# A two-layer hybrid trunk: the third weight sum formed from the second, low products last, block (0,0) summed in PSUM

## The chip, the cores and the metric

One core of one Trainium2 chip. The metric is the device time of one execution in microseconds, the median of the runs. One further execution was profiled; all rows of the trace are from it.

In the profile PE is TensorE's matmul, PEld its weight load, DVE is VectorE, ACT is ScalarE, POOL is GpSimd and SP is SyncE, which only issues transfers here.

## The reference, cut to what matters

Two layers over x, 512 tokens of 1024 numbers, in float32. Each layer is

```
x = x + concat(A, B, C) @ w_out                      # three kinds of attention heads
x = x + relu(RMSNorm(x) @ w_ff1)^2 @ w_ff2           # the feed-forward (FF) part
```

The change lies in the second line: w_ff1 is 1024 x 4096 and w_ff2 is 4096 x 1024, a matrix each per layer.

## The kernel before, in words

**Three products for one.** Float32 operands are split into a high part (rounded to the matmul type fp32r) and a low part (the rest). A product is hi·hi + hi·lo + lo·hi, three matmuls that add up in the same PSUM bank (`mm3`, L260 to L263). The weights are split on the chip: ScalarE copies the raw tile into `whi` (L203), VectorE subtracts that from the raw tile into `wlo` (L204). Both have three buffers (`HIB = 3`).

**Seven products for eight.** Most of the FF part uses a Strassen-Winograd scheme on 2 x 2 blocks, with seven block products. In FF1 the two of the eight slices of w_ff1 that come first (`NSTD = 2`) are done in the plain way, the other six with the scheme. FF2 uses it throughout, in four steps of two groups (`dg` = 0, 1). A *group* is the seven weight tiles A11, S1, S2, A12, S4, S3, A22 (`ORDER`) of 128 x 1024 numbers. There are 14 groups a layer, six of FF1 and eight of FF2, so 28 in all. Of the tiles, A11, A12 and A22 are blocks of the stored matrix (signs are put into the other operand). S1, S2, S3 and S4 are sums:

- S1 = block (1,0) + block (1,1): one plain load by SP's queue, then a second one by GpSimd's queue that adds in the transfer (`load_part`, L152 to L158)
- S2 = S1 + A11: VectorE, in place in A11's slot (L214)
- S4 = S2 + A12: VectorE, in A11's slot (L218)
- S3 = block (0,0) + block (1,0): a plain and an accumulating load
- A22 = block (1,1): a plain load

So a group has five plain loads, two accumulating ones and two VectorE sums, beside the seven splits.

**Jobs.** Each weight tile is a job in one list, in the order of use. `getjob` (L238) hands out the next; `prep_ahead` (L225) prepares up to three jobs ahead (sum if there is one, high part, low part), and `load_ahead` (L170) starts loads, in order, as long as the next one finds a free raw slot. In the FF part there are seven such slots of 128 x 1024 (three `raw`, four in `fraw`). A slot is given back by `drop`: S1's after S2's sum, A12's after S4's sum, A11's after S4's split, S3's and A22's after their own splits.

**The order in the FF part.** After the eight plain jobs, `ff_pairs` alternates a job of FF2 with a job of FF1. FF2 runs over steps, then over the seven products, then over the two groups; FF1 runs over slices, then over the seven products. So 28 jobs, two FF2 groups taken side by side and two FF1 groups one behind the other, are a round. FF1 is through before the last step of FF2, which runs its 14 jobs alone. The list scheduler of the language orders each engine's instructions when the program is built; each engine then works strictly in that order.

**One job on TensorE.** `prod` (L1126) runs over four row tiles and two column halves, with three matmuls of 256 columns each: 24 matmuls, and the low part of the weights comes in with the third.

**FF1's outputs.** `ff1_st` (L1219) does the seven products with banks X, Z and Y. The first product (A11) goes to X and is copied to `ct[:, 0]` in SBUF by ScalarE (L1222); X goes on adding. With the fourth product (A12) in Y, VectorE adds Y to `ct[:, 0]` (L1233), and ScalarE takes relu (L1176) and the square (L1177). Further differences (`n1_`, `n2_`, `tail_`, L1179 to L1190) and splits (L1167, L1168, L1172, L1173) by ScalarE and VectorE make FF2's moving operands. FF2 (`ff2`) adds its banks to xT with VectorE (`acc`, L1265), in the last step with a scaling by r2 (L1267). After layer 0 the next layer's first stage splits xT (L327, L328) and sums its squares (L319 to L323) for a matmul (L455) that takes their mean.

Of the kernel before, what the change touches and what calls it, by code (L numbers as in the profile page):

```python
# [15 lines left out]
AF = mybir.ActivationFunctionType  # L16
ALU = mybir.AluOpType
AX = mybir.AxisListType

P = 128  # L20
# [30 lines left out]
def trunk(ctx, tc, x, cols, rows, gate_w, tabs, w_in, w_out, w1, w2, out):  # L51
    nc = tc.nc
    V, A, G, T = nc.vector, nc.scalar, nc.gpsimd, nc.tensor
# [31 lines left out]
    def wt(tag, name):  # L85
        n, bufs = phase["tags"][tag]
        return phase["pool"].tile([P, n], F32, tag=tag, name=nm(name), bufs=bufs)
# [4 lines left out]
    def smt(n, name):  # L92
        return sm.tile([P, n], F32, tag=f"sm{n}", name=nm(name))

    def v3(a, d=HD):
        return a.rearrange("p (h d) -> p h d", d=d)
# [12 lines left out]
    def st_group(l, blocks):  # L109
        grp = {}  # L110
        for which, ij in (("A11", ((0, 0),)), ("S1", ((1, 0), (1, 1))), ("S2", ()), ("A12", ((0, 1),)), ("S4", ()),
                          ("S3", ((0, 0), (1, 0))), ("A22", ((1, 1),))):
            grp[which] = {"ap": [blocks[i, j] for i, j in ij], "which": which, "grp": grp, "n": 4, "w": 256, "ff": l,
                          "gate": None, "parts": 1}
        return grp
# [51 lines left out]
    def drop(jb):  # L167
        jb["ring"].append(jb.pop("raw"))
# [12 lines left out]
    def hilo():  # L181
        hi = wp.tile([P, D], F32R, tag="whi", name=nm("whi"), bufs=HIB)
        lo = wp.tile([P, D], F32R, tag="wlo", name=nm("wlo"), bufs=HIB)
        return hi, lo

    def prep_part(jb, part):
        if "hl" not in jb:
            jb["hl"] = hilo()
        hi, lo = jb["hl"]
        n, w, raw = jb["n"], jb["w"], jb["raw"]  # L190
        W = w
        if jb["gate"] is not None:
            l, k0 = jb["gate"]
            W = 268
            h3, l3, r3 = v3(hi[:, :n * W], W), v3(lo[:, :n * W], W), v3(raw[:, :n * w], w)
            A.activation(h3[:, :, :w], r3, AF.Copy)
            V.tensor_copy(h3[:, :, w:], gws[l][0][:, k0:k0 + n, :])
            V.tensor_tensor(l3[:, :, :w], r3, h3[:, :, :w], ALU.subtract)
            V.tensor_copy(l3[:, :, w:], gws[l][1][:, k0:k0 + n, :])
        else:  # L200
            m = n * w // jb["parts"]
            cs_ = slice(part * m, (part + 1) * m)
            A.activation(hi[:, cs_], raw[:, cs_], AF.Copy)  # L203
            V.tensor_tensor(lo[:, cs_], raw[:, cs_], hi[:, cs_], ALU.subtract)  # L204
        if part == jb["parts"] - 1:
            jb["res"] = [(hi[:, q * W:(q + 1) * W], lo[:, q * W:(q + 1) * W]) for q in range(n)]
            if jb["which"] in (None, "S3", "A22"):
                drop(jb)

    def prep_job(jb):  # L210
        which, g = jb["which"], jb.get("grp")
        if which == "S2":
            a = jb["raw"] = g["A11"]["raw"]
            V.tensor_tensor(a, g["S1"]["raw"], a, ALU.add)  # L214
            drop(g["S1"])
        elif which == "S4":
            a = jb["raw"] = g["A11"]["raw"]
            V.tensor_tensor(a, g["A12"]["raw"], a, ALU.add)  # L218
            drop(g["A12"])
        for part in range(jb["parts"]):  # L220
            prep_part(jb, part)
        if which == "S4":
            drop(g["A11"])

    def prep_ahead(i):  # L225
        while pos["prep"] < len(jobs):
# [11 lines left out]
    def getjob():  # L238
        i = pos["get"]
        if i > 0:  # L240
            jobs[i - 1].pop("res", None)
        load_ahead(i)
        prep_ahead(i)
        pos["get"] += 1
        return jobs[i]["res"]
# [14 lines left out]
    def mm3(o, sh, sl, mh, ml, first, last, skip=False):  # L260
        T.matmul(o, sh, mh, start=first, stop=False, skip_group_check=skip)  # L261
        T.matmul(o, sh, ml, start=False, stop=False, skip_group_check=skip)  # L262
        T.matmul(o, sl, mh, start=False, stop=last, skip_group_check=skip)  # L263
# [72 lines left out]
    def xop(op, lo):  # L336
        if op < 3:
            i, j = ((0, 0), (1, 0), (1, 1))[op]
            return xb(i, j, xl if lo else xh)
        return xbt["x"][:, ((op - 3) * 2 + lo) * 1024:((op - 3) * 2 + lo + 1) * 1024].rearrange(  # L340
            "p (k q) -> p k q", k=4)
# [54 lines left out]
    def headrms(zt, nh, name):  # L396
        sq = wt("tmp", "hsq")
        A.activation(sq[:, :nh * HD], zt, AF.Square)
        ss = smt(nh, name)
        V.tensor_reduce(ss, v3(sq[:, :nh * HD]), AX.X, ALU.add)  # L400
        v = smt(nh, name + "v")
# [42 lines left out]
    for l in range(L):  # L444
        last = l == L - 1
# [288 lines left out]
        def runA():  # L734
# [7 lines left out]
            def s1(c):  # L742
# [8 lines left out]
                for r in range(2):  # L751
                    V.tensor_reduce(v3(mx, 2)[:, :, r], v3(sc[r], 256)[:, :, :nk], AX.X, ALU.max)
                nmx = smt(4, "nmx")
# [321 lines left out]
        ct, bt = 0, 0  # L1075
# [19 lines left out]
        ct = v3(wt("ct", "ct"), S)  # L1095
# [11 lines left out]
        def bank():  # L1107
            return banks.popleft()
# [16 lines left out]

        def prod(bk, bh, bl, start):  # L1126
            ws = getjob()
            for kk in range(4):
                hi, lo = ws[kk]
                for f in range(2):  # L1130
                    c = slice(f * P, (f + 1) * P)
                    mm3(bk[:, f * 256:(f + 1) * 256], hi[:, c], lo[:, c], bh(kk), bl(kk), start and kk == 0 and f == 0,
                        kk == 3 and f == 1, True)

        def prod1(bk, op, start=True):
            bh, bl = xop(op, 0), xop(op, 1)
            prod(bk, lambda kk: bh[:, kk, :], lambda kk: bl[:, kk, :], start)
# [3 lines left out]
        def prod2(bk, s, op, start=True):  # L1141
            def pick(lo):
                def f(kk):
                    g = GU[s, kk // 2]
                    if op == 0:
                        return g["c"][:, lo, kk % 2, :]
                    tag, a = {1: ("b", 0), 2: ("b", 1), 3: ("n", 0), 4: ("n", 1), 5: ("t", 0), 6: ("t", 1)}[op]
                    return g[tag][lo][:, a, kk % 2, :]
                return f
            prod(bk, pick(0), pick(1), start)  # L1150
# [19 lines left out]
        def csplit(s, rr):  # L1170
            u = GU.setdefault((s, rr), {})["c"] = unit_for(s, False)
            A.activation(u[:, 0], q2(ct[:, 0]), AF.Copy)  # L1172
            V.tensor_tensor(u[:, 1], q2(ct[:, 0]), u[:, 0], ALU.subtract)  # L1173

        def act(a, src, sign):
            A.activation(ct[:, a], src, AF.Relu, scale=sign)  # L1176
            A.activation(ct[:, a], ct[:, a], AF.Square)  # L1177

        def n1_():  # L1179
            V.tensor_tensor(ct[:, 4], ct[:, 0], ct[:, 1], ALU.subtract)  # L1180

        def n2_(s, rr):
            V.scalar_tensor_tensor(ct[:, 5], ct[:, 3], -1.0, ct[:, 4], ALU.mult, ALU.subtract)
            V.tensor_tensor(ct[:, 1], ct[:, 3], ct[:, 1], ALU.subtract)
            gsplit(s, rr, "n", 4)

        def tail_(s, rr):
            gsplit(s, rr, "b", 2)
            V.scalar_tensor_tensor(ct[:, 2], ct[:, 5], -1.0, ct[:, 2], ALU.mult, ALU.subtract)
            gsplit(s, rr, "t", 1)  # L1190
# [26 lines left out]
                    yield  # L1217

        def ff1_st(s, rr):  # L1219
            X = bank()  # L1220
            prod1(X, 0)
            A.activation(ct[:, 0], X, AF.Copy)  # L1222
            yield
            Z = bank()
            prod1(Z, 3)
            A.activation(ct[:, 3], Z, AF.Copy)
            yield
            prod1(X, 4, False)
            A.activation(ct[:, 1], X, AF.Copy)
            yield  # L1230
            Y = bank()
            prod1(Y, 1)
            V.tensor_tensor(ct[:, 0], Y, ct[:, 0], ALU.add)  # L1233
            banks.append(Y)
            act(0, ct[:, 0], 1.0)
            csplit(s, rr)
            yield
            prod1(Z, 2, False)
            V.tensor_tensor(ct[:, 1], Z, ct[:, 1], ALU.add)
            banks.append(Z)  # L1240
            act(1, ct[:, 1], 1.0)
            n1_()
            yield
            prod1(X, 5, False)
            V.tensor_tensor(ct[:, 3], X, ct[:, 3], ALU.add)
            act(3, ct[:, 3], -1.0)
            n2_(s, rr)
            yield
            prod1(X, 6, False)
            act(2, X, -1.0)  # L1250
            banks.append(X)
            tail_(s, rr)
            yield
# [23 lines left out]
        def ff2(s):  # L1277
# [18 lines left out]
            for dg in range(2):  # L1296
                Y = bank()
                prod2(Y, s, 1)
                acc(s, dg, 0, 0, Y, True)
                banks.append(Y)  # L1300
# [102 lines left out]
```

## Time and profile before

| what | value |
|---|---|
| median of 3 runs | 1077.22 us (1075.41 to 1082.15) |
| profiled execution | 1074.93 us, span 1073.2 us |
| matmuls | 8376 |
| transfers that add, GpSimd's queue | 34 into `fraw`, 22 into `raw`, 512 KB each |
| HBM read | 147.86 MB |

A row of the profile that groups instructions reads: line, engine, operation, output <- inputs, shapes, count | busy us, mean ns of one | idle time of the engine before them, and what ended it. A row of the list of waits reads: who waited <- for whom: us in total, times, longest us. A row of the timeline: start, duration, instruction, and in brackets the idle time before it. A matmul's row lasts 0.28 us, but a new one starts every 0.11 us in the FF part, as they are pipelined. Starts of VectorE's neighbouring rows also lie closer than their lengths.

### The profile page before, as it was taken

To read this page: it belongs to the slowest core of one execution; us is meant where nothing else is said; L and a number is where in the kernel's file an instruction comes from. 1 tells how busy PE (TensorE), PEld (TensorE's weight loads), DVE (VectorE), ACT (ScalarE), POOL (GpSimd) and SP (SyncE) were. 2 spreads that over 40 slices of the span, in tenths; PEclk is the share of its full clock that TensorE was granted. 3 is DMA by queue.
4 is the path that set the end of the run, shared out by engine and by line. 5 is a ranking of instruction groups with operands and counts; after the bars stand their busy time and mean duration, and the time that the engine had idled before them with its cause. 6 is when DMAs were issued, how large, how long until landed. Compare 5 with 4: busy or idle time off the path is not lost.

```text
span 1073.2 us, 20903 instructions
## 1 busy us (share of the span) xinstructions
PE 1059.1 (99%) x8376; PEld 989.8 (92%) x8376; DVE 911.9 (85%) x1550; ACT 626.4 (58%) x1097; POOL 103.8 (10%) x154
## 2 busy tenths in 40 slices
PE   8999999999999999999999999999999999999998
PEld 8999977887999999999999998778789999999998
DVE  6696877899997997988977878688999889799897
ACT  5446655376666566566454567444765665576662
POOL 2030020101010010010001200101000100000100
PEclk8999999999999999999999999999999999999999
DMA  6533121145478588588435321213334866876872
GB/s 200 164 110 109 59 68 50 62 174 118 118 197 215 140 213 209 149 210 223 108 108 155 102 80 41 86 44 136 112 87 141 233 178 172 219 183 191 211 185 99
DMA packets 47346, 151.81 MB, mean 141 GB/s; under 512 B 5632, under 2 KB 8832, under 8 KB 47248
## 3 DMA queue, kind: packets, MB, share of 16 engines
q1 hardware_dynamic: 39184, 121.10, 33.8%
q0 software_dynamic: 8064, 29.36, 16.2%
q8 instruction: 66, 1.08, 0.4%
q14 instruction: 32, 0.26, 0.1%
HBM read 147.86 MB, written 2.13 MB: 140 GB/s over the span
## 4 chain that ended last, share of the span: by engine, by line
PE 80%; DVE 11%; ACT 3%; DMA 3%; issue 1%; SPq 0%; DVEq 0%; POOLq 0%
PE at L261 24%; PE at L263 24%; PE at L262 24%; DMA raw<-in_w_dram 3%; DVE wlo L204 2%; DVE rt L719 2%; PE at L849 1%; PE at L891 1%; PE at L874 1%; ACT whi L203 1%; ACT pe L762 1%; PE at L972 1%; DVE yg L1168 1%; DVE z L715 1%; DVE z L721 1%
## 5 line engine op out<-in xcount | busy, mean ns | idle before, releaser
L203 ACT ACTIVATE whi<-raw 128x1024 fp32r<-128x1024 f32 (+1 forms) x144 | 150.9, 1048 | 143.7 <-PE at L262 103.2
L204 DVE TENSOR_TENSOR wlo<-raw,whi 128x1024 fp32r<-128x1024 f32 (+1 forms) x144 | 173.8, 1207 | 41.2 <-ACT whi L203 40.7
L203 ACT ACTIVATE whi<-fraw 128x1024 fp32r<-128x1024 f32 x122 | 129.2, 1060 | 92.4 <-PE at L262 76.2
L261 PE MATMUL at<-yg,whi 128*128 128x256 f32 (+1 forms) x592 | 179.8, 307 | 0.0
L263 PE MATMUL at<-yg,wlo 128*128 128x256 f32 (+1 forms) x592 | 178.4, 301 | 0.0
L262 PE MATMUL at<-xhl,whi 128*128 128x256 f32 (+1 forms) x576 | 177.9, 309 | 0.0
L262 PE MATMUL at<-yg,whi 128*128 128x256 f32 (+1 forms) x560 | 169.6, 303 | 0.0
L261 PE MATMUL at<-whi,xhl 128*128 128x256 f32 (+1 forms) x576 | 164.1, 285 | 2.1 <-ACT whi L203 1.3
L262 PE MATMUL at<-wlo,xhl 128*128 128x256 f32 (+1 forms) x576 | 161.5, 280 | 0.3 <-DVE wlo L204 0.3
L263 PE MATMUL at<-whi,xhl 128*128 128x256 f32 (+1 forms) x576 | 161.5, 280 | 0.0
L261 PE MATMUL at<-xhl,whi 128*128 128x256 f32 (+1 forms) x512 | 161.1, 315 | 0.0
L263 PE MATMUL at<-xhl,wlo 128*128 128x256 f32 (+1 forms) x512 | 160.3, 313 | 0.0
L204 DVE TENSOR_TENSOR wlo<-fraw,whi 128x1024 fp32r<-128x1024 f32 x122 | 148.9, 1221 | 8.6 <-ACT whi L203 8.1
L261 PEld LDWEIGHTS at<-yg,whi 128*128 128x128 f32 x592 | 111.2, 188 | 5.6 <-issue 1.7
L263 PEld LDWEIGHTS at<-yg,wlo 128*128 128x128 f32 x592 | 111.2, 188 | 5.3
L262 PEld LDWEIGHTS at<-xhl,whi 128*128 128x128 f32 x576 | 108.0, 188 | 7.6 <-issue 0.5
L261 PEld LDWEIGHTS at<-whi,xhl 128*128 128x128 f32 x576 | 109.4, 190 | 3.2 <-ACT whi L203 1.6
L262 PEld LDWEIGHTS at<-wlo,xhl 128*128 128x128 f32 x576 | 109.5, 190 | 0.5 <-DVE wlo L204 0.5
L263 PE MATMUL at<-xbx,wlo 128*128 128x256 f32 x384 | 106.6, 278 | 3.4 <-DVE wlo L204 3.4
L263 PEld LDWEIGHTS at<-whi,xhl 128*128 128x128 f32 x576 | 109.3, 190 | 0.3 <-DVE xhl L328 0.3
L262 PEld LDWEIGHTS at<-yg,whi 128*128 128x128 f32 x560 | 105.3, 188 | 4.2 <-DVE yg L1002 0.5
L261 PE MATMUL at<-xbx,whi 128*128 128x256 f32 x384 | 106.1, 276 | 0.0
(286 smaller groups left out, 2423.1 us busy)
## 6 DMA issues: line engine op xcount, KB each, us to landing
fraw<-in_w_dram SPq DMA_DIRECT2D x90, 512.0 KB, 4.5
raw<-in_w_dram SPq DMA_DIRECT2D x66, 512.0 KB, 4.5
raw<-in_w_in_dram SPq DMA_DIRECT2D x34, 512.0 KB, 3.4
fraw<-in_w_dram POOLq DMA_DIRECT2D x34, 512.0 KB, 6.0
raw<-in_w_dram POOLq DMA_DIRECT2D x22, 512.0 KB, 7.9
raw<-in_w_out_dram SPq DMA_DIRECT2D x16, 512.0 KB, 3.4
rowb<-drow SPq DMA_DIRECT2D x16, 256.0 KB, 4.0
raw<-in_w_in_dram SPq DMA_DIRECT2D x12, 256.0 KB, 3.8
```

Of the source, the lines that this page charges most:

```text
L203: A.activation(hi[:, cs_], raw[:, cs_], AF.Copy)
L204: V.tensor_tensor(lo[:, cs_], raw[:, cs_], hi[:, cs_], ALU.subtract)
L261: T.matmul(o, sh, mh, start=first, stop=False, skip_group_check=skip)
L262: T.matmul(o, sh, ml, start=False, stop=False, skip_group_check=skip)
L263: T.matmul(o, sl, mh, start=False, stop=last, skip_group_check=skip)
L715: V.tensor_tensor(z10, z10, bc(rq), ALU.mult)
L719: V.tensor_tensor(r10[:, oo:oo + n, a:a + 32], z10[:, oo:oo + n, b:b + 32], tb(S_, n, a, a + 32), ALU.mult)
L721: V.tensor_tensor(zaq[t], ro[:, :640], rt[:, :640], ALU.add)
L762: A.activation(pe[:, u, :nk], sc[u % 2][:, (u // 2) * 256:(u // 2) * 256 + nk], AF.Exp, bias=nmx[:, u:u + 1], accum_out=ssum[:, u:u + 1])
L849: T.matmul(sp[:, :nk], qTB[rs, pr, n * P:(n + 1) * P], kTB[rs, pr, :nk], start=True, stop=False)
L874: T.transpose(pt[:, b * P:(b + 1) * P], scs[r][:, b * P:(b + 1) * P], ident)
L891: T.matmul(pobs[pr][r * 64:(r + 1) * 64, n * P:(n + 1) * P], zbv[b][:, h * 64:(h + 1) * 64], ps[r][:, b * P:(b + 1) * P], start=b == 0, st ...
```

## The change

S3 is no longer loaded. As S2 = (0,0) + (1,0) + (1,1), VectorE subtracts block (1,1) from S2, in A11's slot, which is held until S3's split. Block (1,1) is A22's tile, so its load moves up to S3's place in the list, and job A22 loads nothing. S4's sum goes into A12's slot in place of A11's, since S2 is still wanted. `prod` does the high part's 16 matmuls first, then the low part's 8. In `ff1_st`, ScalarE copies X to bank Y, and the A12 product adds to it there; VectorE's addition goes.

```diff
@@ st_group
-                          ("S3", ((0, 0), (1, 0))), ("A22", ((1, 1),))):
+                          ("S3", ((1, 1),)), ("A22", ())):
@@ prep_part
-        n, w, raw = jb["n"], jb["w"], jb["raw"]
+        n, w, raw = jb["n"], jb["w"], jb.get("src", jb.get("raw"))
...
-            if jb["which"] in (None, "S3", "A22"):
+            if jb["which"] is None:
                 drop(jb)
@@ prep_job
-        if which == "S2":
-            a = jb["raw"] = g["A11"]["raw"]
-            V.tensor_tensor(a, g["S1"]["raw"], a, ALU.add)
-            drop(g["S1"])
-        elif which == "S4":
-            a = jb["raw"] = g["A11"]["raw"]
-            V.tensor_tensor(a, g["A12"]["raw"], a, ALU.add)
-            drop(g["A12"])
+        last = None
+        if which:
+            a = g["A11"].get("raw")
+            jb["src"] = a if which in ("S2", "S3") else jb["raw"] if "raw" in jb else None
+            if which == "S2":
+                V.tensor_tensor(a, g["S1"]["raw"], a, ALU.add)
+                drop(g["S1"])
+            elif which == "S4":
+                jb["src"], last = g["A12"]["raw"], g["A12"]
+                V.tensor_tensor(jb["src"], jb["src"], a, ALU.add)
+            elif which == "S3":
+                V.tensor_tensor(a, a, jb["raw"], ALU.subtract)
+                last = g["A11"]
+            elif which == "A22":
+                jb["src"], last = g["S3"]["raw"], g["S3"]
         for part in range(jb["parts"]):
             prep_part(jb, part)
-        if which == "S4":
-            drop(g["A11"])
+        if last:
+            drop(last)
@@ prod
-            for kk in range(4):
-                hi, lo = ws[kk]
-                for f in range(2):
-                    c = slice(f * P, (f + 1) * P)
-                    mm3(bk[:, f * 256:(f + 1) * 256], hi[:, c], lo[:, c], bh(kk), bl(kk), start and kk == 0 and f == 0,
-                        kk == 3 and f == 1, True)
+            for i in range(2):
+                for kk in range(4):
+                    for f in range(2):
+                        c, o = slice(f * P, (f + 1) * P), bk[:, f * 256:(f + 1) * 256]
+                        w = ws[kk][i][:, c]
+                        T.matmul(o, w, bh(kk), start=start and i == kk == f == 0, stop=i == 1 and kk == 3,
+                                 skip_group_check=True)
+                        if i == 0:
+                            T.matmul(o, w, bl(kk), start=False, stop=False, skip_group_check=True)
@@ ff1_st
-            X = bank()
+            X, Y = bank(), bank()
             prod1(X, 0)
-            A.activation(ct[:, 0], X, AF.Copy)
+            A.activation(Y, X, AF.Copy)
...
-            Y = bank()
-            prod1(Y, 1)
-            V.tensor_tensor(ct[:, 0], Y, ct[:, 0], ALU.add)
+            prod1(Y, 1, False)
+            act(0, Y, 1.0)
             banks.append(Y)
-            act(0, ct[:, 0], 1.0)
```

## The prediction

> **What bounds the kernel now.** I read the page's busy table first, then the list of waits, then busy time by stretches, and last the timeline at one stall. An FF *job* is one weight tile of 24 matmuls; seven jobs make a group; a *round* is two FF2 groups and two FF1 groups taken in turn, 28 jobs.
>
> ```profile
> span 1073.2 us, 20903 instructions
> ...
> PE 1059.1 (99%) x8376; PEld 989.8 (92%) x8376; DVE 911.9 (85%) x1550; ACT 626.4 (58%) x1097; POOL 103.8 (10%) x154
> ```
>
> TensorE is idle for 14 us of 1073. The waits of TensorE, then those of the engines that feed it:
>
> ```profile
> PE at L263 <- DVE wlo L204: 3.4, 4, 1.1
> PE at L261 <- ACT whi L203: 1.3, 1, 1.3
> ```
> ```profile
> ACT whi L203 <- PE at L262: 179.4, 140, 4.2
> ...
> DVE wlo L204 <- ACT whi L203: 48.8, 73, 4.8
> ...
> ACT whi L203 <- DMA raw<-in_w_dram: 12.5, 4, 5.0
> ...
> DVE raw L214 <- DMA raw<-in_w_dram: 3.6, 3, 1.3
> ```
>
> The largest wait of TensorE is for low parts (wlo), 3.4 us in four places. ScalarE, which makes the high parts, waits 179 us for TensorE to free a buffer: the preparation normally runs ahead and is held back by TensorE. The stretches:
>
> ```profile
> 270.00:280.00 10.00, 9.36 (x82) 9.16 (x81) 9.72 (x11) 8.80 (x10) 0.00 (x0) 1.00 0.00 0
> ```
> ```profile
> 350.00:360.00 10.00, 8.95 (x79) 8.75 (x79) 8.67 (x10) 5.59 (x7) 0.00 (x0) 1.00 0.53 112
> 430.00:440.00 10.00, 8.97 (x79) 8.78 (x78) 10.00 (x11) 5.64 (x7) 0.86 (x1) 1.00 0.40 119
> 800.00:810.00 10.00, 9.35 (x82) 9.15 (x81) 9.71 (x12) 8.33 (x10) 0.00 (x0) 1.00 0.03 9
> ```
> ```profile
> 356.50:434.00 77.50, 76.47 (x673) 76.28 (x673) 68.12 (x73) 48.61 (x59) 6.93 (x8) 1.00 0.73 191
> ...
> 500.00:545.00 45.00, 45.00 (x396) 44.87 (x395) 44.45 (x56) 26.29 (x32) 2.26 (x3) 1.00 0.45 115
> ...
> 810.00:1068.00 258.00, 258.00 (x2267) 257.72 (x2266) 228.13 (x246) 153.87 (x181) 21.69 (x25) 1.00 0.69 186
> ```
>
> Columns: length, then busy time of TensorE, its weight loads, VectorE, ScalarE, GpSimd, clock, DMA share, GB/s. The first four rows hold the four stalls. The last row is almost the whole second FF stage without an idle moment of TensorE: 258/2267 = 0.114 us a matmul, 2.73 us a job. The fifth row is one round: VectorE is busy 68.1 of 77.5 us, so 9.4 us are free. In the sixth, the end of the first FF stage, VectorE is full. So TensorE's matmul count sets the time, the change leaves that count alone, and only stalls can be won or made.
>
> **The stalls and the late low parts.** One stall, on TensorE and on VectorE:
>
> ```profile
> 355.15 0.28 PE L262 MATMUL at<-xbx,whi 128*128 128x256 f32 x1
> 356.48 0.39 PE L263 MATMUL at<-xbx,wlo 128*128 128x256 f32 x1 [1.05 <-DVE wlo L204]
> ```
> ```profile
> 349.17 1.22 DVE L204 TENSOR_TENSOR wlo<-fraw,whi 128x1024 fp32r<-128x1024 f32 x1
> 351.73 1.23 DVE L214 TENSOR_TENSOR raw<-raw,raw 128x1024 f32<-128x1024 f32 x1 [1.33 <-DMA raw<-in_w_dram]
> 352.87 1.22 DVE L1168 TENSOR_TENSOR yg<-ct,yg 128x1024 fp32r<-128x1024 f32 x1
> 354.00 0.68 DVE L1265 TENSOR_TENSOR xT<-xT,at 128x512 f32<-128x512 f32 x1
> 354.60 0.69 DVE L1189 SCALAR_TENSOR_TENSOR ct<-ct 128x512 f32<-128x512 f32 x1
> 355.20 1.22 DVE L204 TENSOR_TENSOR wlo<-fraw,whi 128x1024 fp32r<-128x1024 f32 x1
> ```
>
> VectorE held a sum (L214) that stood waiting for a load, then FF1's bookkeeping, and only then the low part that the third matmul of the job needs. The high part was there: two matmuls of the job ran. Start to start the stall is 356.48 - 355.15 = 1.33 us where 0.11 is normal: 1.2 us. For all four: idle 3.4 plus, each, the 0.28 - 0.114 = 0.17 that the row's length overlaps: **4.05 us**. No stall is over 1.2 us.
>
> With low products last, TensorE needs the low part at the 17th matmul and not the 3rd: 14 x 0.114 = 1.59 us later, more than the worst lateness. I therefore take -4.05 us. Bounds: 0, if what is added on VectorE makes the low parts later by as much, and -4.05, since the FF stages hold no other stall. The high buffer's last reader becomes matmul 16 and not 23, so ScalarE may start 0.8 us earlier; it is ahead already, and I price that at 0.
>
> **VectorE's added and removed work.** Durations by line, first in the round above, then over the run:
>
> ```profile
> L204 DVE TENSOR_TENSOR wlo<-fraw,whi 128x1024 fp32r<-128x1024 f32 x17 | 20.8, 1221 | 1.2 <-ACT whi L203 1.1
> ...
> L214 DVE TENSOR_TENSOR fraw<-fraw 128x1024 f32<-128x1024 f32 x3 | 3.7, 1224 | 0.6 <-DMA fraw<-in_w_dram 0.5
> ...
> L1233 DVE TENSOR_TENSOR ct<-at,ct 128x512 f32<-128x512 f32 x2 | 1.4, 692 | 0.4 <-PE at L263 0.2
> ```
>
> The new subtraction has the shape of L214: 1.22 us, and 1.14 from start to start where such instructions follow each other (349.17 to the next was a wait; 351.73 to 352.87 is 1.14). There are 28 groups (14 a layer): +32 us. The removed addition L1233 runs 12 times, 0.69 us, 0.60 start to start (354.00 to 354.60): -7 us. A round gets 4 x 1.14 - 2 x 0.60 = +3.4 us against 9.4 free; with the 1.2 us stall gone the round is shorter and 4.8 us stay free. Beside TensorE, so 0 on the path, while it is spread. A job's low part is normally ready well before its job, as high copies start when TensorE frees the buffer of three jobs back: that leaves 2 x 2.73 - 1.06 (copy) - 1.22 = 3.2 us, and now 1.59 more. That cover hides four such subtractions in a row; without it each would cost its 1.14 us. S3's preparation becomes VectorE, ScalarE, VectorE in a chain, as S2's and S4's are, which cause no wait of TensorE by themselves.
>
> **Loads, slots, queues.**
>
> ```profile
> fraw<-in_w_dram SPq DMA_DIRECT2D x90, 512.0 KB, 4.5
> ...
> fraw<-in_w_dram POOLq DMA_DIRECT2D x34, 512.0 KB, 6.0
> raw<-in_w_dram POOLq DMA_DIRECT2D x22, 512.0 KB, 7.9
> ```
> ```profile
> L158 POOL DMA_DIRECT2D fraw<-in_w_dram x34: 856/865/1013, 244.1 to 1029.1; - x34
> ...
> DMA to landing us min/median/max: 3.1/5.5/10.4
> ```
>
> A group's five plain loads become four and its two accumulating ones become one: 28 of 56 issues leave GpSimd's queue and 28 leave SP's. TensorE never waits for a load directly, so they win 0; the stall above began with a load, but an S1 one, which stays. In exchange A11's slot is held until S3 and block A22's slot until A22. Counting the ring of seven slots through the job order, FF2's second group now finds the slot for its S3 load 4 jobs ahead (6 before), the others 6 or 7: 4 x 2.73 = 10.9 us, against a median landing of 4.5 and a longest of 10.4. I price it at 0; the bounds are 0 and the rival below.
>
> [...]
>
> **Block (0,0) in PSUM.** X is still copied once by ScalarE, into another bank; the addition leaves VectorE; relu reads PSUM.
>
> ```profile
> L1222 ACT ACTIVATE ct<-at 128x512 f32<-128x512 f32 x12 | 6.9, 578 | 0.0
> ```
>
> A write to PSUM by ScalarE is not in these rows; from the nearest, 0.58 us to SBUF, I take 0.58 (bounds 0 and twice that), off the path. The bank is held from FF1's first job to its fourth: FF1 has three and FF2 five, all eight, but in the order of the jobs no bank is reused sooner than three jobs (8.2 us) after its last reader, a 0.68 us addition. Price 0.
>
> **The end of the first FF stage.** VectorE has no room from 500 to 545. The last two groups add 2 x 1.14 = 2.3 us there. What is late next:
>
> ```profile
> 543.78 0.68 DVE L1267 TENSOR_TENSOR xT<-xT,r 128x512 f32<-128x512 f32 x1
> ...
> 548.56 3.73 DVE L323 TENSOR_TENSOR accs<-accs,sq 128x512 f32<-128x512 f32 x5
> ```
> ```profile
> 552.68 0.50 PE L455 MATMUL at<-ones_m,accs 128*128 128x1 f32 x4
> ```
>
> The last scaling frees the buffer in which the next layer's squares are summed; that sum ends at 552.3 and TensorE reads it at 552.7, 0.4 us of margin. Shifted by 2.3, TensorE stands 1.9 us at L455, once. Bounds 0 (the planner may put the scaling ahead of low parts) and 2.3. I take **+1.9**. At the very end nothing is due:
>
> ```profile
> 1065.69 0.69 DVE L1265 TENSOR_TENSOR xT<-xT,at 128x512 f32<-128x512 f32 x1 [1.30 <-PE at L263]
> ```
>
> There VectorE waits for TensorE again, 1.3 us twice.
>
> **Sum.** -4.05 + 1.9 = -2.15 us. The profiled execution took 1074.93 us (span 1073.2 and 1.7 around it): 1072.8. The median of the runs is 1077.22, 2.3 above it; on that scale, **1075.0 us**.
>
> **Rivals.** *The stalls only move*: VectorE's order is planned anew, another sum stands ahead of a low part, and nothing is won: 1077. For it: four stalls came from that order; against: 1.59 us of new cover. *The whole gain*: no stall at L455, 1073.2. *VectorE's queue stands behind loads*, the slower side: VectorE works in order, and the new subtraction waits for block A22's landing with everything queued behind it (low parts, FF2's additions). It decides from a mean of 4.8/4 = 1.2 us a subtraction on. At 2 us, a round loses 4 x 2 - 4.8 = 3.2, six rounds 19 us: 1096. For it: L214 waited 1.2 us on average, and S3 loads have made ScalarE wait up to 5.0; against: the load is now plain, and 10.9 us ahead at the least. [...]
>
> **How the numbers follow.** Forecast 0.50, whole gain 0.15, stalls move 0.20, port lock 0.02, VectorE behind loads 0.11, and 0.02 for a gain that I do not see. 1% (10.8 us) is about what a measurement of this kernel can tell from no change: faster by that 0.02, same 0.87, slower 0.11. Low end: the whole gain, 1073.2, less the 1.8 by which the fastest run shown lies under the median: 1071. High end: no gain at the slowest run, 1082.2, and the start of the loads' rival (1.5 us a subtraction: 1.2 x 6 = 7): 1084.
>
> **What would show it.** Right: no wait of TensorE for wlo in the FF stages; 28 accumulating issues; VectorE about 25 us busier; a wait of TensorE at the L455 matmuls near 1.9 us. Wrong: waits of the new subtraction for DMA above 1.2 us on average, or FF stretches with under 87 matmuls in 10 us.

## The result, and the profile after

The changed kernel takes **1093.01 us** (median of 6 runs, 1084.09 to 1095.9). Six runs of before beside it give 1076.32 us (1071.6 to 1082.15). The quotient of these medians is 1.0155; the ratio, which here and below leaves out runs more than 1.5% above the fastest of their kernel, is 1.0127 with a 95% interval of 1.0085 to 1.0169. That is slower by 1.3%, where 1075.0 us and a range of 1071 to 1084 were forecast. The profiled execution has a span of 1093.0 us, 19.8 more than before's 1073.2.

The page's busy table:

```profile
span 1093.0 us, 20783 instructions
...
PE 1067.9 (98%) x8376; PEld 998.5 (91%) x8376; DVE 930.6 (85%) x1566; ACT 623.4 (57%) x1097; POOL 77.6 (7%) x126
```

The edit itself is all there: 16 more VectorE instructions (28 subtractions less 12 additions), 28 fewer GpSimd issues, as many matmuls as before. TensorE's busy time cannot show what was lost, as the rows overlap (0.28 us long, a new one every 0.113 us in the FF stages). The list of TensorE's waits shows it (who <- for whom: us in total, times, longest):

```profile
PE at L1140 <- DVE wlo L204: 13.0, 4, 4.9
```

Before had 3.4 us for low parts, four times, 1.1 at most. There are still four places, but now up to 4.9 us each. VectorE's own waits say why the low parts are late:

```profile
DVE raw L217 <- DMA fraw<-in_w_dram: 14.7, 2, 7.6
...
DVE raw L217 <- DMA raw<-in_w_dram: 9.7, 2, 4.9
```

L217 is the sum S2 (L214 before), an instruction that the change did not touch in substance. It waited 3.6 and 0.5 us before and waits 24.4 us now. The new subtraction (L223) waits for no transfer at all. VectorE around the first of the four waits:

```profile
341.45 1.22 DVE L204 TENSOR_TENSOR wlo<-raw,whi 128x1024 fp32r<-128x1024 f32 x1
350.30 1.23 DVE L217 TENSOR_TENSOR raw<-fraw,raw 128x1024 f32<-128x1024 f32 x1 [7.63 <-DMA fraw<-in_w_dram]
...
353.24 1.23 DVE L1178 TENSOR_TENSOR gx<-ct,gx 128x1024 fp32r<-128x1024 f32 x1
354.39 2.35 DVE L204 TENSOR_TENSOR wlo<-fraw,whi 128x1024 fp32r<-128x1024 f32 x2
```

The same place before, from the low part of the same FF2 job A11 on. The prediction's rows of 349.17 (a low part) and 351.73 (the sum in question) follow these:

```profile
342.62 1.23 DVE L204 TENSOR_TENSOR wlo<-raw,whi 128x1024 fp32r<-128x1024 f32 x1 [0.29 <-ACT whi L203]
...
345.61 1.22 DVE L204 TENSOR_TENSOR wlo<-fraw,whi 128x1024 fp32r<-128x1024 f32 x1
```

Before, two low parts (345.61 and 349.17) stood between A11's low part and this sum. After the change the sum stands directly behind A11's low part, ahead of those two. The other three long waits are of the same kind: each is at the S2 sum of FF2's first group, in its second or third step, and each of these sums stands two low parts earlier than before. The load that it needs came no later than before. GpSimd issued its adding transfer in the changed kernel (first row) 1.8 us earlier than before (second row):

```profile
339.18 0.86 POOL L158 DMA_DIRECT2D fraw<-in_w_dram  x1 [1.99 <-DMA fraw<-in_w_dram]
```
```profile
341.02 0.87 POOL L158 DMA_DIRECT2D raw<-in_w_dram  x1 [2.26 <-DMA raw<-in_w_dram]
```

From issue to landing it took 11.0 us after the change and 10.7 before; why it takes so long at this place stays open. VectorE works in order, so it stood at the sum for 7.63 us, and the two low parts behind it came at 354.39. TensorE, in the job that wanted the first of them:

```profile
350.50 0.28 PE L1143 MATMUL at<-xhl,whi 128*128 128x256 f32 x1
355.66 1.73 PE L1140 MATMUL at<-xhl,wlo 128*128 128x256 f32 x8 [4.88 <-DVE wlo L204]
357.19 0.41 PE L1140 MATMUL at<-xhl,whi 128*128 128x256 f32 x1
357.40 0.41 PE L1143 MATMUL at<-xhl,whi 128*128 128x256 f32 x1
...
359.53 0.28 PE L1143 MATMUL at<-yg,whi 128*128 128x256 f32 x1
```

All 16 matmuls of the high part are done, as the new product order wants it, and still the low part is 5 us away. Behind the pause the matmuls start 0.21 us apart instead of 0.113 until 359.5. The stretches of TensorE (length, busy and rows, clock, DMA share, GB/s) show that and one thing more:

```profile
300.00:350.00 50.00, 50.00 (x443) 1.00 0.58 156
...
356.10:359.50 3.40, 3.40 (x18) 0.50 0.00 0
360.20:430.00 69.80, 69.80 (x595) 1.00 0.48 135
448.00:545.00 97.00, 97.00 (x826) 1.00 0.38 114
```

The granted clock fell to one half for 3.4 us after this pause, and again after the one of 4.56 us at 893 us; the pauses of 2.07 and 2.35 us had no such stretch. And from 360 to 545 us, but for some 9 us behind the second pause, a matmul took 97.0/826 = 0.1174 us, though the clock is 1.00 and nothing waits; ahead of the first pause it was 50.0/443 = 0.1129. (From start to start in the timeline it is 0.1178 and 0.1133; these two are used below.)

So the 19.8 us are, by an estimate from this one execution: pauses 13.0 and 4 x 0.17 of overlap, 13.7 against before's 4.05, +9.6; two stretches of 3.4 us at half clock, each 3.4 x (1 - 0.113/0.213) = 1.6, +3.2; some 173 us at 0.1178 instead of 0.1133 us a matmul, 6.6, against 25 us of that in before (1.0), +5.6. That is 18.4 of 19.8.

### The profile page after: what moved, and what is told of

The parts are those of the page before. It is cut to its first block, busy times and chain, and to the rows that moved or that the text cites. A ratio compares the mean times of both kernels' runs of the same rounds, so it can differ in the third digit from the quotient of the medians.

```text
span 1093.0 us, 20783 instructions
## 1 busy us (share of the span) xinstructions
PE 1067.9 (98%) x8376; PEld 998.5 (91%) x8376; DVE 930.6 (85%) x1566; ACT 623.4 (57%) x1097; POOL 77.6 (7%) x126
## 4 chain that ended last, share of the span: by engine, by line
PE 76%; DVE 11%; DMA 6%; ACT 4%; issue 2%; SPq 0%; DVEq 0%; ACTq 0%; POOLq 0%
PE at L1140 28%; PE at L1143 14%; PE at L268 9%; PE at L270 9%; PE at L269 9%; DMA fraw<-in_w_dram 3%; DMA raw<-in_w_dram 2%; DVE wlo L204 2%; DVE rt L726 2%; PE at L856 1%; PE at L898 1%; PE at L881 1%; ACT whi L203 1%; ACT pe L769 1%; PE at L979 1%
## 5 line engine op out<-in xcount | busy, mean ns | idle before, releaser
L204 DVE TENSOR_TENSOR wlo<-raw,whi 128x1024 fp32r<-128x1024 f32 (+1 forms) x150 | 180.9, 1209 | 18.6 <-ACT whi L203 18.4
L203 ACT ACTIVATE whi<-fraw 128x1024 fp32r<-128x1024 f32 x116 | 122.1, 1055 | 91.6 <-PE at L1143 50.1
L204 DVE TENSOR_TENSOR wlo<-fraw,whi 128x1024 fp32r<-128x1024 f32 x116 | 140.6, 1221 | 8.0 <-ACT whi L203 7.2
L1140 PE MATMUL at<-yg,whi 128*128 128x256 f32 x464 | 111.8, 280 | 0.5 <-DVE xT L1273 0.5
L1143 PE MATMUL at<-yg,whi 128*128 128x256 f32 x432 | 103.9, 279 | 0.0
L1143 PE MATMUL at<-xhl,whi 128*128 128x256 f32 x416 | 100.2, 280 | 0.0
L1140 PE MATMUL at<-xbx,whi 128*128 128x256 f32 x384 | 90.6, 278 | 0.0
L1143 PE MATMUL at<-xbx,whi 128*128 128x256 f32 x384 | 90.4, 278 | 0.0
L1140 PEld LDWEIGHTS at<-yg,whi 128*128 128x128 f32 x464 | 88.2, 190 | 0.9 <-DVE xT L1273 0.7
L1140 PE MATMUL at<-gx,whi 128*128 128x256 f32 x368 | 88.1, 278 | 0.0
L1140 PE MATMUL at<-xhl,whi 128*128 128x256 f32 x352 | 84.7, 281 | 0.0
L1143 PEld LDWEIGHTS at<-yg,whi 128*128 128x128 f32 x432 | 82.0, 190 | 0.0
L1143 PE MATMUL at<-gx,whi 128*128 128x256 f32 x336 | 80.4, 278 | 0.0
L1143 PEld LDWEIGHTS at<-xhl,whi 128*128 128x128 f32 x416 | 79.4, 191 | 0.0
L1273 DVE TENSOR_TENSOR xT<-xT,at 128x512 f32<-128x512 f32 x112 | 76.6, 684 | 2.5 <-PE at L1140 1.9
```

Source lines behind the costliest of these rows:

```text
L1140: T.matmul(o, w, bh(kk), start=start and i == kk == f == 0, stop=i == 1 and kk == 3, skip_group_check=True)
L1143: T.matmul(o, w, bl(kk), start=False, stop=False, skip_group_check=True)
L1273: V.tensor_tensor(t_, t_, q2(bk), ALU.subtract if i else ALU.add)
```

## The experiments

Each kernel was compared with runs of before beside it, on one chip: `e1` to `e4` on one, with before at 1080.23 us, `e5` to `e8` on a second (1074.32), `e9` to `e11` on a third (1076.37), `e12` to `e15` on the first again (1078.38). Small differences are read within one of these groups. Theory A: the products' order alone makes the list scheduler move one S2 sum forward, and it waits there for the adding transfer. Rival B: the third sum's work and slots. Rival C: chance. Rival D, for block (0,0): the bank. In the expectations from `e5` on, the letters mean what is said there.

**One edit at a time.** `e1`: `prod` as changed, the rest as before.

> Before with one of the three edits alone: the low parts' products come last in each job; weight sums and block (0,0) as before. Theory A (order): this edit alone makes the scheduler put the second sum of the group of FF2 d0 two low parts earlier in VectorE's fixed order, where the accumulating load of S1 has not landed; the trace should show VectorE waiting about 7 us twice and about 5 us twice for that load at the sum, four pauses of TensorE for low parts of 2 to 5 us, and a half-clock window after the two long ones: 1085 to 1094 us, slower than before by 10 to 17 us. Rival B (third sum): the slowdown belongs to VectorE's 32 us of added sums and to the slots held longer; then this kernel has none of it and shows the gain forecast for it, 1071 to 1076 us. Rival C (chance: spells at 118 ns a matmul fall into some runs): within 5 us of before, and no wait at the second sum over 2 us.

1096.41 us (1090.48 to 1099.82), ratio 1.0165 (1.0128 to 1.0203). Its waits of TensorE and of VectorE:

```profile
PE at L1133 <- DVE wlo L204: 13.5, 4, 3.9
```
```profile
DVE raw L214 <- DMA raw<-in_w_dram: 24.4, 4, 6.6
```

The whole loss, with 24.4 us of waiting at the sum, comes with the products' order alone. It was even a little more than the 1085 to 1094 us expected.

`e2`: the third sum by VectorE alone (`st_group`, `prep_part`, `prep_job` as changed, `prod` and `ff1_st` as before).

> Before with the third weight sum by VectorE alone; the products' order and block (0,0) as before. Theory A (order): the second sums keep their places in VectorE's order, so no long wait for the accumulating load; 28 accumulating transfers go away and VectorE gains 28 subtractions (32 us) that lie beside TensorE: 1073 to 1080 us, within 4 us of before. Rival B (third sum): this edit is the cause: 1085 to 1095 us, with waits of VectorE at the new subtraction or at the sums of 5 us and more. Rival C: within 5 us of before.

1082.04 us (1074.42 to 1088.53), ratio 1.0022 (0.9988 to 1.0056): no difference that can be measured. No pause of TensorE in its FF stages reaches 1 us, though the profiled run, at 1088.53 us, is the slowest of the twelve (its slow matmuls are shown in the last section). Rival B does not account for the loss.

`e3`: block (0,0) in PSUM alone (`ff1_st`).

> Before with block (0,0) summed in PSUM alone: one addition of VectorE a round less, the copy of product 0 goes to PSUM. Theory A and rival B: no effect, 1074 to 1079 us. Rival D (the PSUM bank held longer, or the copy into PSUM, is the cause): 1085 us or more, with TensorE waiting for a bank or for ScalarE in the FF1 rounds.

1077.59 us, ratio 1.0000 (0.997 to 1.0029). Rival D falls.

**Theory A from the side of the order.** `e4` is the changed kernel with one constraint on the scheduler: the S2 sum comes behind the low part of the job prepared just ahead of it.

```diff
-            V.tensor_tensor(lo[:, cs_], raw[:, cs_], hi[:, cs_], ALU.subtract)
+            marks_lo[0] = V.tensor_tensor(lo[:, cs_], raw[:, cs_], hi[:, cs_], ALU.subtract).ins
...
-                V.tensor_tensor(a, g["S1"]["raw"], a, ALU.add)
+                with tc.issue_after(marks_lo[0]):
+                    V.tensor_tensor(a, g["S1"]["raw"], a, ALU.add)
```

> The changed kernel with all three edits, and the second sum fixed in VectorE's order behind the low part of the job ahead of it. Theory A (order): VectorE's waits of 5 to 8 us for the accumulating load at the second sum go, the four pauses of TensorE of 2 to 5 us and the two half-clock windows go with them: 1068 to 1077 us, faster than the changed kernel by 15 to 20 us. Rival B (third sum): the loads are still late, the wait shows at another instruction, 1085 us or more. Rival C: 1080 to 1095 us with spells of slow matmuls and no waits.

1074.99 us, and 12 runs lie within 1073.98 to 1076.41; ratio 0.9971 (0.9947 to 0.9995). No wait of VectorE for weight transfers is left, nor of TensorE for low parts in the FF stages. One constraint took away some 17 us (1.0127 to 0.9971 of before), and rival C falls with it.

**Theory A from the side of the load.** `e9` keeps VectorE's early order as it is, but makes S1 a single plain load. It leaves out the second block, so its sums lack that block and only its time is of use:

```diff
-("S1", ((1, 0), (1, 1)))
+("S1", ((1, 0),))
```

> The changed kernel, VectorE's order as it is, with S1 left as its first block alone: the accumulating load of the second block is left out (28 transfers on POOL's queue), so the sums that use it lack that block. Theory A (the early second sum waits because the accumulating transfer lands 10 to 11 us after its issue): with a plain load, which lands 3 to 4 us after issue, the same early place costs little: VectorE's waits at the second sum fall from 24.4 us to under 4 us, no pause of TensorE over 2 us in the FF stages, 1070 to 1078 us. Rival (the early place harms by itself, because it delays low parts queued behind it, whether the load is there or not): the pauses stay at 2 us and more and it is 1083 to 1095 us.

1070.98 us (1070.41 to 1072.22), ratio 0.9938 (0.9909 to 0.9967). The same sum, in the same early place, in the rows of VectorE for S2 and the low parts:

```profile
340.18 1.22 DVE L204 TENSOR_TENSOR wlo<-raw,whi 128x1024 fp32r<-128x1024 f32 x1
341.43 1.22 DVE L217 TENSOR_TENSOR raw<-fraw,raw 128x1024 f32<-128x1024 f32 x1
```

It starts without a wait at 341.43, where it stood until 350.30 in the changed kernel. The loads are the difference: a plain one lands a median of 3.3 us after issue here, and in the changed kernel GpSimd's adding ones took

```profile
DMA to landing us min/median/max: 5.3/6.4/11.0
```

beside the plain load that has to land first. So the early place is harmful because of the load, and the load because of the early place; either remedy is enough. Taking out the adding loads also takes 28 transfers off the queues, so `e9` does not tell the adding transfer's own slowness from the traffic around it.

**What the edits are worth without the waits.** `e5` is `e4` with the third sum given back to the transfers, `e7` is before with the constraint alone, and `e10` adds the products' order to `e7` without block (0,0).

> The kernel with all three edits and the fixed place of the second sum, but with the third weight sum given back to the accumulating transfers, as in before. It asks what the third sum costs once the long waits are gone. In the run with the fixed place TensorE still paused at the end of both FF stages, about 3.4 us between 527 and 537 us and 1.6 us between 1057 and 1062 us, for parts that VectorE and ScalarE delivered late while VectorE had no gap between 512 and 541 us. Theory A (VectorE's 28 subtractions fill its queue there): those pauses shrink to under 1.5 us in all, 1068 to 1072.5 us, faster than with the third sum by 2 to 6 us. Rival B (the added 32 us cost nothing, as the forecast had it; the late sums come from the fixed place itself): the pauses stay, 1073.5 to 1076.5 us. Rival C (the accumulating transfers for S3 land late): 1077 us or more with waits of VectorE for them.

1070.05 us (1068.96 to 1071.28), ratio 0.9948 (0.9922 to 0.9974). The end of the first FF stage in `e4`, then in `e5` (length, then busy time of TensorE, its weight loads, VectorE, ScalarE, GpSimd):

```profile
512.00:541.00 29.00, 26.69 (x227) 25.90 (x226) 28.99 (x38) 13.75 (x17) 0.53 (x1) 1.00 0.17 56
```
```profile
512.00:541.00 29.00, 29.00 (x249) 29.00 (x247) 28.29 (x39) 16.62 (x23) 0.53 (x1) 1.00 0.38 114
```

VectorE is without a gap in `e4` (28.99 of 29.00), and TensorE pauses four times:

```profile
528.49 0.39 PE L1142 MATMUL at<-yg,whi 128*128 128x256 f32 x1 [0.95 <-ACT whi L204]
531.73 0.50 PE L270 MATMUL at<-whi,xhl 128*128 128x256 f32 x2 [0.24 <-ACT whi L204]
532.70 0.38 PE L1142 MATMUL at<-yg,whi 128*128 128x256 f32 x1 [0.47 <-DVE xT L1275]
536.36 0.38 PE L1142 MATMUL at<-yg,whi 128*128 128x256 f32 x1 [0.65 <-DVE xT L1275]
```

The first waits for a high part whose raw tile VectorE's subtraction delivered late, the last two for FF2's additions to xT. In `e5` none of these is there.

> Before, with nothing changed but the fixed place of the second sum behind the low part of the job ahead. Theory A (the long waits of the changed kernel come from the reordering alone): before's order was not far off, so little changes: the four pauses for low parts at the FF1 jobs (0.5 to 1.3 us each) stay or go singly, 1070 to 1080 us. Rival (the fixed place is a gain of its own, whatever the products' order): 1066 to 1070 us.

1072.25 us (1071.54 to 1076.68), ratio 0.9982 (0.996 to 1.0005): the constraint alone is not a gain that can be measured. `e5` ran on the same chip, and all its runs lie under all of `e7`: 2.2 us for the products' order and block (0,0) together, with the sum in this tight place, directly behind the low part of the job ahead.

> Before with the low parts' products last and the second sum's fixed place; third sum and block (0,0) as before. It differs from the version at 1070.05 us only in block (0,0), and from before with the fixed place (1072.25 us) only in the products' order. If block (0,0) in PSUM costs and gains nothing: 1069 to 1071 us. If the 28 fewer instructions' worth of VectorE time there (an addition of 0.7 us in each of 12 rounds) was part of the gain: 1071 to 1073 us. If the products' order gained nothing by itself: 1072 us and more.

1070.94 us (1069.75 to 1081.1), ratio 0.9979 (0.9941 to 1.0017): near `e5`, as block (0,0) without effect would have it; a difference under 1 us between two chips is not read.

**A looser constraint.** `e6` is `e4`, `e11` is `e5`, each with the sum behind the low part of three jobs back (`marks_lo` as a list, `marks_lo[-3]`).

> The changed kernel with the second sum fixed behind the low part of three jobs back instead of the job just ahead. Theory A: the waits for the accumulating load stay under 1 us, and the pauses at the end of the FF stages stay as they were if VectorE's added work makes them (1073 to 1076 us), or go if the tight fixed place made them (1069 to 1072.5 us). If three jobs are too early again, VectorE waits 2 us and more for the load and it is 1077 us or more.

1072.02 us (1071.24 to 1072.47), ratio 0.9977 (0.9955 to 0.9999), in the range given for pauses that the tight place makes; yet TensorE still waits 1.9 us for additions to xT, 1.5 of it in one piece.

> The version at 1070.05 us (no third sum by VectorE, second sum fixed) with the second sum behind the low part of three jobs back instead of one, which with the third sum brought 1074.99 to 1072.02 us. If the remaining pauses near 510 and 1037 us (0.3 us each, and the slow cadence behind the first) come from the tight place: 1067 to 1069.5 us. If not: 1069.5 to 1071 us. If three jobs is too early for the load: 1072 us and more with waits of VectorE.

1068.53 us (1068.17 to 1077.57), ratio 0.9939 (0.9907 to 0.9972), the fastest so far. Three jobs back is not too early: it puts the four sums behind the same low parts as before had them (read in the rows of `e13`, the same kernel). VectorE waits for transfers a little, and TensorE does not wait for a low part in this profile.

```profile
DVE fraw L221 <- DMA raw<-in_w_dram: 3.2, 2, 1.7
...
DVE fraw L217 <- DMA fraw<-in_w_dram: 2.6, 3, 1.4
```

**The sizes, on one chip.** `e12` is `e6` again, `e13` is `e11`, `e15` is `e4`, and `e14` is before with the sum three jobs back.

> The changed kernel with the second sum fixed three jobs back, once more, beside the version without the third sum on one chip: the versions compared so far ran on three different chips (74.99 and 72.02 against 70.05 and 68.53, all over 1000 us), so a difference of 2 to 5 us might be the chips'. If the third sum costs on the path by itself, this is 2.5 to 4.5 us slower than the version without it; if the chips made the difference, within 1 us of it.

1071.32 us (1070.34 to 1072.68), ratio 0.9947 (0.9921 to 0.9973).

> The second sum fixed three jobs back, low products last, block (0,0) in PSUM, third sum by the transfers: the partner of the run before. Third sum costly: 2.5 to 4.5 us faster than that. Chips: within 1 us.

**1068.84 us** (1067.6 to 1070.84), ratio 0.9913 (0.9887 to 0.9939). The third sum costs 1071.32 - 1068.84 = 2.5 us. Most of it is in TensorE's waits for FF2's additions to xT, in `e12`, then in `e13`; the two long ones of `e12` end at 531.39 and 534.96 us, at the end of the first FF stage:

```profile
PE at L1143 <- DVE xT L1276: 2.0, 3, 1.5
```
```profile
PE at L1136 <- DVE xT L1269: 0.2, 1, 0.2
```

This version, with low products last, block (0,0) in PSUM, S3 by the transfers and the sum kept three jobs back, is faster than before, and than the changed kernel by more than the chips differ.

> The changed kernel with the second sum fixed behind the job just ahead, beside the looser place on the same chip. If the tight place itself delays parts at the end of the FF stages: 2 to 4 us slower than the looser one. If the chips made that difference: within 1 us.

1074.78 us (1073.96 to 1075.51): the tight place costs 3.5 us beside `e12`. So the pauses of `e4` came from both the third sum and the tight place.

> Before with the second sum fixed three jobs back and nothing else changed. Its distance to the run before is what the products' order and block (0,0) gain once no wait is in the way: 4.05 us if the forecast of that term was right in size, 1 to 3 us if the fixed place alone already takes most of the four pauses, 0 or less if the order of the products has no worth of its own.

1081.29 us (1072.25 to 1083.1), ratio 1.0033 (0.9998 to 1.0068). That is 12.4 us over `e13`, more than any of the three readings foresaw. Three runs lie at 1072.3 to 1072.7, the other nine at 1080.0 to 1083.1. The profiled execution is one of the nine. Its waits for low parts are small:

```profile
PE at L265 <- DVE wlo L205: 1.7, 3, 0.6
```

but the matmuls of the first FF stage are slow from 300 to 500 us, while those of the second are not:

```profile
300.00:500.00 200.00, 200.00 (x1700) 1.00 0.74 197
...
810.00:1030.00 220.00, 218.86 (x1928) 1.00 0.72 193
```

0.1176 us each against 218.86/1928 = 0.1135. Over these 200 us that is, by estimate, 200 x (1 - 0.1133/0.1178) = 7.6 us. This execution lies 7.7 us above the three, the median of the nine 10.0. That the three are runs without such a stretch is likely, but only one of the twelve was traced. Against the three, picked after the fact, the products' order and block (0,0) gain some 3.5 us.

**The slow matmuls.** `e8` puts twelve short dependencies into `e4`, one in each Strassen round of FF1:

```diff
             A.activation(Y, X, AF.Copy)
+            p = 7 * (2 * s + rr - NSTD) + 1
+            g = GU[p // 14, 0]
+            m = (g["b"][0][:, 1, 0, 0:1] if (p % 14) // 2 else g["c"][:, 0, 0, 0:1])
+            A.activation(m, X[:, 0:1], AF.Identity, bias=m.bitcast(F32), scale=0.0)
```

> The changed kernel with the fixed place, and six times in each FF stage a short dependency on purpose: a ScalarE instruction on one column of the next product's operand that must wait for the product before (the value is kept: column plus zero times the product). Each should hold TensorE 0.4 to 1.2 us, 12 times, 5 to 14 us in all. In the traces so far every stretch with matmuls 117.8 ns apart instead of 113.3 ns in the FF stages begins and ends at a short hold or pause of TensorE. Theory A (after a hold TensorE resumes in one of two cadences and keeps it until the next hold): some of the 12 stretches of about 36 us run at 117.8 ns (1.4 us more each), and the runs scatter over more than 5 us where the kernel without the holds scattered over 2.4 us in 12 runs: 1080 to 1098 us. Rival D (the slow cadence has another cause, chance in time or heat): every stretch at 113.3 ns or one long spell that ignores the holds, scatter under 3 us, 1080 to 1089 us.

1086.0 us in 6 runs, 1083.37 to 1092.1: the scatter of 8.7 us is what theory A asked for. But in the profiled execution the three stretches measured between the holds (twelve in both stages, 4.2 us idle together and 0.5 at most) did not run slowly:

```profile
278.20:316.40 38.20, 38.20 (x338) 1.00 0.37 111
317.60:355.20 37.60, 37.60 (x333) 1.00 0.62 168
356.40:394.10 37.70, 37.70 (x334) 1.00 0.38 113
```

They took 0.113 us a matmul. A hold, then, can be followed by slow matmuls, as the one of 0.1 us at 447.6 us in the changed kernel (0.1178 us behind it), but needn't be.

## Why the prediction was wrong, point by point

**The stalls, -4.05 us: the step that failed.** The text read one stall rightly (a sum that waits for an S1 load, with a low part behind it) and then kept VectorE's order fixed while TensorE's was changed. It gave the term bounds of 0 and -4.05, "if what is added on VectorE makes the low parts later by as much". The order is made by a list scheduler for all engines together. With low products last, its order has this sum two low parts earlier, and the real transfer was not there; what the scheduler assumed for the transfer is not on record. So a third bound was missing, that of a longer stall: the term measured +9.6 us in pauses, and +3.2 in half clock behind them. `e1`, `e4` and `e9` show it from three sides. The 1.59 us of cover fit the runs once the sum's place was fixed: products' order and block (0,0) gain 2.2 us in the tight place (`e5` against `e7`) and 3.5 in the loose one against the three faster runs of `e14`, where 4.05 were forecast. Against the median of `e14` it is 12.4, much of it slow matmuls (7.6 us by estimate in the profiled run), for which the forecast had no term.

**"Only stalls can be won or made."** This premise left two things out. Of the 19.8 us, 3.2 are half clock behind pauses and 5.6 are matmuls 0.1178 instead of 0.1133 us apart, which no wait shows.

**The rivals.** *The stalls only move* had the mechanism, in the words "VectorE's order is planned anew, another sum stands ahead of a low part". It priced it at no change, as if a moved stall kept its size. Its size is that of the transfer that the sum then meets: up to 11.0 us from issue to landing in the changed kernel, of which 7.6 were left to wait at the sum and 4.9 on TensorE. *VectorE's queue stands behind loads* had the sign and nearly the time (1096), but at the wrong instruction: it put the wait at the new subtraction, and the trace has it at S2, with none at the subtraction; that the time came out near is luck. The decision point given (a mean wait of 1.2 us per subtraction) never came into play. *The port lock*, the rival of chance 0.02 in which VectorE's added sums make S1's adding transfers later, is shown by no run: the adding transfers took a median of 6.4 us from issue to landing in the changed kernel (6.7 before, S3's among them), their issues 853 to 1013 ns (856 to 1013 before), and `e2`, with all the added sums, has no pause of 1 us.

**VectorE's +32 us beside TensorE, 0 on the path.** With before's order of the products it cannot be told from zero (`e2`, 1.0022, 0.9988 to 1.0056). Without the long waits it is 2.5 us (`e12` against `e13`), lost where the prediction saw that VectorE has no room, at the end of the first FF stage. There the term was mis-sized. Busy time rose by 18.7 us, where about 25 was written.

**The end of the first FF stage, +1.9 us at L455.** The changed kernel's list of waits has no entry for that line's successor (L462), and only 0.5 us for an addition to xT. So the term measured nothing in the kernel it was meant for, where TensorE was late already. In the versions without the long waits VectorE's shortage shows, but a little earlier than the text had it, at the jobs of the last FF2 step (the rows of `e4` and `e12`), where no margin had been worked out. That its size in `e12`, 2.0 us, is near 1.9 is luck.

**Loads and slots 0, block (0,0) 0.** Both held: no wait for an S3 load, and `e3` at 1.0000. ScalarE's copy from PSUM to PSUM took a median of 580 ns, as taken.

**What would show it.** 28 adding issues: right. No wait for wlo: wrong, 13.0 us, and that line alone would have told. Of the two signs of being wrong, waits of the subtraction did not show; stretches with under 87 matmuls in 10 us did (595 in 69.8 us, 85), but from the slow spacing and not from loads.

## What to carry to other kernels

Where a scheduler writes each engine's order at build time, a change in one engine's instructions can move another engine's. After such an edit, compare the orders, and look at every instruction that waits for a transfer: how long is its transfer in the trace, and what stands behind it on its engine. If the plan and the landing disagree, one explicit constraint on that instruction can be worth more than the edit: here it took away some 17 us, and with it, and with the third sum given back, stands a version 0.9% faster than before (`e13`, 0.9887 to 0.9939; `e11`, the same kernel on another chip, 0.6%). Price a moved stall by the wait that it meets in the new place, and not by its old size.

## What the runs showed of the hardware

A pause of TensorE can cost more than its length. In the changed kernel, after the pauses of 5.16 and 4.56 us the granted clock was 0.50 for 3.4 us each, 1.6 us more. In `e1` a pause of 3.77 us from start to start (3.49 us idle in the first row, and the 0.28 of a matmul's row) was followed by a longer stretch at half clock,

```profile
349.00:353.00 4.00, 0.51 (x5) 0.83 0.09 17
353.00:358.40 5.40, 5.40 (x26) 0.50 0.00 0
435.00:439.00 4.00, 3.66 (x32) 1.00 0.01 4
```

while the one that ends at 435.3, of 3.69 us at the least (13.5 us idle in four pauses, the others at most 3.49, 2.70 and 3.9), was followed by none (third row). A shorter one, of 2.98 us (2.70 us idle), was followed by half clock again: a mean of 0.77 over 7.3 us is 3.4 us at one half.

```profile
887.00:894.30 7.30, 4.60 (x26) 0.77 0.02 4
```

So the length of a pause does not tell by itself whether half clock follows; what decides it is not shown here.

The other finding has no explanation here. In the FF stages matmuls follow each other either 0.1133 or 0.1178 us apart, with the granted clock at 1.00 and no wait. In `e2` and `e4`, over long stretches without a pause:

```profile
360.00:540.00 180.00, 180.00 (x1530) 1.00 0.41 118
...
900.00:1080.00 180.00, 180.00 (x1531) 1.00 0.42 120
```
```profile
290.00:500.00 210.00, 210.00 (x1855) 1.00 0.51 144
810.00:1030.00 220.00, 220.00 (x1944) 1.00 0.50 142
```

0.1176 against 0.1132 us, 4%. In the FF stages of `before` and of the changed kernel there are three such stretches of over 5 us. In the changed kernel one begins with the change of clock at 359.5 us and lasts until the pause at 436.3 us; the next begins behind two matmul starts 0.22 us apart, at 447.56 us, and lasts to the end of the stage. In `before` one begins behind two starts 0.25 us apart, at 936.37 us, and lasts until two that are 0.19 us apart, at 962.04 us. The reverse does not hold. Behind the stall of 1.33 us at 355.15 us in `before` the matmuls were 0.1133 us apart, behind the change of clock at 902.2 us and the pause of 2.35 us up to 978.1 us in the changed kernel 0.1133 and 0.1135, and between `e8`'s holds 0.113. Outside the FF stages such a start is not needed: in `before`, the next layer's first products run slowly from 540.3 us on, with no start more than 5 ns out of step in the 2.5 us ahead of it. So such a stretch can cost 7.6 us (`e14`, by estimate) that no list of waits shows, but that a hold causes it is not shown, and which of the two spacings follows stays open. `e15` scatters little, 1073.96 to 1075.51 us, where the runs of before in its ratio lie at 1071.18 to 1086.89; but `e11`, with few waits too, has two of twelve runs 9 us above the others.
